# A hybrid S5 / sparse-attention trunk: the adaLN blocks get other places in a hand-written filling plan

## Chip, core and metric

One NeuronCore of a Trainium2 chip runs the whole program. The metric is the device time of one execution in microseconds (us). The kernel before takes 1371.88 us (median of 3 runs, 1369.35 to 1375.03).

## What is computed

Two layers over a residual stream x of 256 positions and 2048 channels. Layer 0 is an S5 state-space mixer, layer 1 a native-sparse-attention mixer (NSA). Every sub-layer is preceded by an RMSNorm whose output is modulated by a conditioning vector c (adaLN). Cut to what matters:

```
c_act = silu(c)
shift, scale, gate = split(c_act @ mod_w[layer] + mod_b[layer], 3)     # layers 0 and 1
h = rmsnorm(x) * (1 + scale) + shift
# layer 0
u, z = split(h @ w_in, 2)
y = gelu(scan(u) + d_skip * u)            # diagonal complex state space, 128 groups
x = x + gate * ((y * sigmoid(y @ w_glu + b_glu) * silu(z)) @ w_out)
# seam: shared keys and values
kv_shift, kv_scale = split(c_act @ kv_mod_w + kv_mod_b, 2)
kv = (rmsnorm(x) * (1 + kv_scale) + kv_shift) @ w_kv        # then compressed blocks
# layer 1
q, gates, z = split(h1 @ w_qg); o = sum(gates * silu(z) * attention branches)
x = x + gate1 * (o @ w_o);  result = rmsnorm(x)
```

The adaLN products are matrix times vector: every 128 outputs need a 2048 x 128 block of weights, 1 MB, used once.

## The kernel before, in words

**Layout.** x is held transposed, 128 channels by 256 positions in each of 16 tiles. A projection (project, L235) makes 128 outputs from 16 tiles: its weights come in two halves of 512 KB on SP's queue (load_w, L187), each half is split into a high and a low part, 4 tiles at a time (split_w, L195: ACT writes hi at L203, DVE writes lo at L204), and TensorE does three matmuls per tile (L231 to L233): 48 matmuls of 128x256 for one block.

**The ring.** All weights, those of the projections and those of adaLN, go through one pool of 8 buffers of 512 KB (raw_tile, L95; bufs=8 at L77). A transfer is issued when a buffer is free. The hi and lo tiles have 4 buffers each (L78).

**adaLN blocks have two forms.** Columns of c_act @ mod_w needed by the first projection (32 blocks) are made in the prologue. The other 96 blocks are spread over the rest of the kernel:

- dve_mod (L138), letter "d": one block on VectorE. Two transfers of 512 KB on SP's queue, and for each a scalar_tensor_tensor in place over 128x1024 with an accumulated sum (L145). It takes two ring buffers until DVE has used them. It needs cact, the broadcast silu(c), which is loaded and made at L546 and L547, inside the S5 stage.

```
            for e in range(2):
                r = raw_tile()
                nc.sync.dma_start(r, mt[i][:, 8 * e:8 * e + 8, :])
                rf = r.rearrange("p a b -> p (a b)")
                nc.vector.scalar_tensor_tensor(out=rf, in0=rf, scalar=1.0, in1=cact[:, 1024 * e:1024 * e + 1024],
                                               op0=OP.mult, op1=OP.mult,
                                               accum_out=modw[:, col - 32:col - 31] if e else modv[:, col:col + 1])
```

- pe_mod (L169), letter "m": a pair of blocks on TensorE (pe_mod_pair, L150). Four transfers of 512 KB, 32 matmuls of 128x128 (L158; fp32, so the trace counts 64), a copy by ACT (L161), two small matmuls (L163), two bias additions by ACT (L166). There is one PSUM tile for it, so one pair follows the other.

The constants NA and NB (L40) say how many of the 32 blocks for the keys and values, and of the 32 for layer 1's shift and scale, are made in pairs; PE_MODS and DVE_MODS are the orders in which they are made. In all there are 8 pairs and 80 "d".

**Stages.** Prologue with the first 8 blocks of u (to about 157 us in the trace). S5 stage: the u blocks that are left (letter "u", one half of a projection), a turn of u into the scan's layout by 32 KB transfers that ACT and POOL issue (u_turn, L555 to L561), scan_in (L601, TensorE), scan_run (L630, a chain on DVE), scan_local, a second turn and the same for the second half (f=1), scan_out (L677), y_turn (L698), y_split; meanwhile the z blocks ("z", one half each). Then a loop over the z blocks that are left (L738), GLU (16 projections, L746), output (16 projections, L762), the norm between the layers (the seam, L778 to L783), 24 key/value projections (L917) with 8 pieces of compression ("c") and 16 rows of the first q blocks ("q", L886), 12 q projections (L977), 16 heads (L986), and the last projection.

**The plan.** fill() (L596) is called at 119 places; each call takes the next string of PLAN (L59) and issues its letters there:

```
    def fill():
        for c in PLAN[slot[0]]:
            {"u": u_half, "z": z_half, "m": pe_mod, "d": dve_mod, "c": lambda: cmp_next(), "q": lambda: q_rows()}[c]()
        slot[0] += 1
```

The string behind the second turn and that of the z loop are two of them; the loop spreads its "m" and "d" over its blocks (L736). Deadlines are caught up in code: 16 "d" before the output stage (L757), all blocks for keys and values before the seam (L771 to L774), and in q_rows the blocks that its row needs (L894 to L898):

```
        while npe[0] < NA + min(NB, 2 * k + 2):
            pe_mod()
        if 2 * k >= NB:
            while ndve[0] < 48 - NA + 2 * k + 2 - NB:
                dve_mod()
```

The text's order is a priority: the framework that builds the program puts an instruction ahead of an earlier one on the same engine where it expects the earlier one to wait. On the chip each engine then runs its instructions in the order so fixed.

Of the kernel before, what the change touches and what calls it, by code (L numbers as in the profile page):

```python
# [36 lines left out]

NA, NB = 12, 4  # L40
L1 = [t for k in range(16) for t in (48 + k, 64 + k)]
PE_MODS = list(range(96, 96 + NA)) + L1[:NB]
DVE_MODS = list(range(32, 48)) + list(range(96 + NA, 128)) + L1[NB:] + list(range(80, 96))
# [3 lines left out]
def spread(n, slots, a=0):  # L47
# [9 lines left out]


PLAN = [  # L59
# [1106 lines left out]
```

## Time and profile before

| what | value |
|---|---|
| median of 3 runs | 1371.88 us (1369.35 to 1375.03) |
| profiled execution, device time | 1371.4 us |
| its span, first to last instruction | 1369.4 us |
| busy PE / DVE / ACT | 1262.9 / 1060.8 / 675.8 us |
| read from HBM | 324.79 MB |
| mean granted TensorE clock | 0.962 of full speed |

The profiled execution lies 0.5 us under the median; 2.0 us of it are outside the span. Busy time of PE is that of pipelined matmuls whose ends are modelled, so what PE can do is better read from the spacing of its starts.

### The profile page before, as it was taken

To read this page: it belongs to the slowest core of one execution; us is meant where nothing else is said; L and a number is where in the kernel's file an instruction comes from. 1 tells how busy PE (TensorE), PEld (TensorE's weight loads), DVE (VectorE), ACT (ScalarE), POOL (GpSimd) and SP (SyncE) were. 2 spreads that over 40 slices of the span, in tenths; PEclk is the share of its full clock that TensorE was granted. 3 is DMA by queue.
4 is the path that set the end of the run, shared out by engine and by line. 5 is a ranking of instruction groups with operands and counts; after the bars stand their busy time and mean duration, and the time that the engine had idled before them with its cause. 6 is when DMAs were issued, how large, how long until landed. Compare 5 with 4: busy or idle time off the path is not lost.

```text
span 1369.4 us, 31323 instructions
## 1 busy us (share of the span) xinstructions
PE 1262.9 (92%) x12266; PEld 1211.3 (88%) x12266; DVE 1060.8 (77%) x2303; ACT 675.8 (49%) x1446; POOL 66.7 (5%) x139
## 2 busy tenths in 40 slices
PE   2799989799989999988998899999999999999994
PEld 1687889798889999988998899999999999999994
DVE  5999558889867887879876789877888777776664
ACT  3255554336454555444444455555555556565652
POOL 2000224120010000000000000000000000000001
PEclk9899989899999999998889999999999999999997
DMA  9799864447888999988886789876565444444541
GB/s 341 253 378 316 317 213 149 123 161 249 306 281 285 344 367 368 367 332 297 274 264 219 237 287 369 314 270 227 176 200 195 145 155 151 144 153 155 185 139 62
DMA packets 97347, 334.43 MB, mean 244 GB/s; under 512 B 14560, under 2 KB 15488, under 8 KB 96176
## 3 DMA queue, kind: packets, MB, share of 16 engines
q1 hardware_dynamic: 91792, 321.45, 66.9%
q0 software_dynamic: 4384, 9.94, 2.2%
q8 instruction: 96, 1.57, 0.5%
q10 hardware_dynamic: 1024, 1.05, 0.3%
q14 instruction: 51, 0.42, 0.1%
HBM read 324.79 MB, written 4.19 MB: 240 GB/s over the span
## 4 chain that ended last, share of the span: by engine, by line
PE 75%; DMA 10%; DVE 9%; issue 3%; ACT 2%; ACTq 1%; SPq 0%; DVEq 0%
PE acc L233 20%; PE acc L231 20%; PE acc L232 19%; DMA raw<-in_mt_dram 5%; DVE lo L204 2%; PE macc L158 2%; DMA mraw<-in_m0n_dram 2%; DVE raw L145 2%; PE s L1000 1%; PE tp L670 1%; PE vp L612 1%; PE op L1051 1%; DMA U<-x 1%; PE uacc L302 1%; ACTq L561 1%
## 5 line engine op out<-in xcount | busy, mean ns | idle before, releaser
L203 ACT ACTIVATE hi<-raw 128x512 fp32r<-128x512 f32 x640 | 398.7, 630 | 464.0 <-PE acc L232 395.4
L204 DVE TENSOR_TENSOR lo<-raw,hi 128x512 fp32r<-128x512 f32 x640 | 431.8, 687 | 144.6 <-ACT hi L203 139.3
L232 PE MATMUL acc<-hq,hi 128*128 128x256 f32 x960 | 274.2, 286 | 0.0
L231 PE MATMUL acc<-hq,hi 128*128 128x256 f32 x960 | 273.1, 285 | 0.0
L233 PE MATMUL acc<-hq,lo 128*128 128x256 f32 x960 | 270.4, 283 | 0.0
L145 DVE SCALAR_TENSOR_TENSOR raw<-raw,ey 128x1024 f32<-128x1024 f32 x160 | 194.6, 1220 | 54.5 <-DMA raw<-in_mt_dram 51.9
L232 PEld LDWEIGHTS acc<-hq,hi 128*128 128x128 f32 x960 | 181.0, 188 | 3.6 <-issue 3.3
L231 PEld LDWEIGHTS acc<-hq,hi 128*128 128x128 f32 x960 | 181.0, 189 | 1.0 <-issue 1.0
L233 PEld LDWEIGHTS acc<-hq,lo 128*128 128x128 f32 x960 | 180.3, 189 | 0.7 <-issue 0.7
L233 PE MATMUL acc<-hkv,lo 128*128 128x256 f32 x384 | 116.9, 305 | 11.0 <-DVE lo L204 10.9
L232 PE MATMUL acc<-hkv,hi 128*128 128x256 f32 x384 | 114.8, 300 | 4.9 <-DVE hkv L266 4.7
L231 PE MATMUL acc<-hkv,hi 128*128 128x256 f32 x384 | 115.2, 301 | 3.6 <-ACT hi L203 3.3
L233 PE MATMUL acc<-h,lo 128*128 128x256 f32 x384 | 112.6, 294 | 4.0 <-DVE lo L204 4.0
L231 PE MATMUL acc<-h,hi 128*128 128x256 f32 x384 | 114.2, 298 | 0.0
L232 PE MATMUL acc<-h,hi 128*128 128x256 f32 x384 | 111.3, 290 | 0.0
L233 PEld LDWEIGHTS acc<-hkv,lo 128*128 128x128 f32 x384 | 79.7, 208 | 14.2 <-DVE lo L204 13.8
L232 PEld LDWEIGHTS acc<-hkv,hi 128*128 128x128 f32 x384 | 79.4, 207 | 6.3 <-DVE hkv L266 6.3
L231 PEld LDWEIGHTS acc<-hkv,hi 128*128 128x128 f32 x384 | 79.4, 207 | 4.9 <-ACT hi L203 4.9
L233 PEld LDWEIGHTS acc<-h,lo 128*128 128x128 f32 x384 | 75.4, 197 | 6.4 <-DVE lo L204 5.0
L158 PE MATMUL macc<-mraw,cz 128*32 128x128 f32 x1536 | 57.2, 300 | 24.0 <-DMA mraw<-in_m0n_dram 20.0
L231 PEld LDWEIGHTS acc<-h,hi 128*128 128x128 f32 x384 | 75.8, 197 | 2.5 <-issue 1.0
L232 PEld LDWEIGHTS acc<-h,hi 128*128 128x128 f32 x384 | 75.9, 198 | 0.2 <-issue 0.2
(332 smaller groups left out, 2827.0 us busy)
## 6 DMA issues: line engine op xcount, KB each, us to landing
raw<-in_mt_dram SPq DMA_DIRECT2D x160, 512.0 KB, 6.0
raw<-in_w_z_dram SPq DMA_DIRECT2D x96, 512.0 KB, 3.8
mraw<-in_m0n_dram SPq DMA_DIRECT2D x64, 512.0 KB, 8.0
raw<-in_w_in_dram SPq DMA_DIRECT2D x48, 512.0 KB, 4.4
raw<-in_w_kv_dram SPq DMA_DIRECT2D x48, 512.0 KB, 5.0
mraw<-in_mn_dram SPq DMA_DIRECT2D x32, 512.0 KB, 6.0
raw<-in_w_glu_dram SPq DMA_DIRECT2D x32, 512.0 KB, 5.8
raw<-in_w_out_dram SPq DMA_DIRECT2D x32, 512.0 KB, 7.5
```

The source lines that it names most:

```text
L145: nc.vector.scalar_tensor_tensor(out=rf, in0=rf, scalar=1.0, in1=cact[:, 1024 * e:1024 * e + 1024], op0=OP.mult, op1=OP.mult, accum_out=mo ...
L158: nc.tensor.matmul(acc[32 * j:32 * j + 32, 128 * e:128 * e + 128], cz[:, q, :], r[:, q % 8, :], start=(e == 0 and q < 4), stop=(q >= 12), ...
L203: nc.scalar.activation(hi[:, 0:c, :], rr, AF.Copy)
L204: nc.vector.tensor_sub(lo[:, 0:c, :], rr, hi[:, 0:c, :].bitcast(F32))
L231: nc.tensor.matmul(acc, hi[:, kk, :], act(0, k), start=(k == 0), stop=False)
L232: nc.tensor.matmul(acc, hi[:, kk, :], act(1, k), start=False, stop=False)
L233: nc.tensor.matmul(acc, lo[:, kk, :], act(0, k), start=False, stop=(k == KT - 1))
L302: nc.tensor.matmul(acc, hi[:, i % 4, :], h0(0, k), start=(k == 0 and i % 2 == 0), stop=False, skip_group_check=True)
L561: (nc.gpsimd if e else nc.scalar).dma_start(U[o:o + 16, f, g], ucm[f][32 * g + 16 * e:32 * g + 16 * e + 16, j])
L612: nc.tensor.matmul(p[e][64 * g2:64 * g2 + 64, hl, r, :], VH[pr, r, h].rearrange("p b m -> p (b m)")[:, 64 * g2:64 * g2 + 64], U[pr, f, 2 * ...
L670: nc.tensor.matmul(p[pr, m, :], tz[pr, hl].rearrange("p d n m -> p (d n) m")[:, :, m], U[pr, f, 2 * g2 + hl, m, :], start=(m == 0), stop=T ...
L1000: nc.tensor.matmul(sp, qo(a, h)[:, qs], kk[:, kv, b, o:o + w], start=(i == 0), stop=(i == 2))
```

## The change

Two constants and the first half of the plan change; no function does. NA goes from 12 to 8 and NB from 4 to 8: of the 16 blocks that are made in pairs, 4 move from the keys and values to layer 1, and as many the other way among the "d". The number of pairs (8) and of "d" (80) stays.

```diff
-NA, NB = 12, 4
+NA, NB = 8, 8
 PLAN = [
-    "uduudu", "u", "u", "u", "u", "uuuu", "uu", "uu", "zzzz", "z", "z", "z", "z", "z", "z", "zzzz", "zz",
-    "z", "z", "z", "z", "zz", "d", "d", "d", "", "d", "", "d", "zzzzddddm",
-    "d", "d", "d", "d", "m", "d", "d", "d", "d", "d", "m", "d", "d", "d", "d", "m",
-    "d", "d", "d", "d", "m", "d", "d", "d", "d", "m", "d", "d", "d", "", "d", "",
-    "mm",
+    "ududuududu", "ud", "u", "ud", "u", "uudu", "uu", "ud", "zzdzzzzd", "zd", "z", "zd", "z", "zd", "z", "zzdz", "zzd",
+    "z", "zd", "z", "zd", "zz", "d", "d", "d", "", "d", "", "d", "zzzzdddd",
+    "d", "", "d", "", "m", "d", "", "d", "", "d", "m", "d", "", "d", "", "d",
+    "m", "d", "", "d", "d", "", "d", "", "m", "d", "d", "", "d", "", "d", "d",
+    "mmmm",
     "d", "d", "d", "d", "dcd", "dc", "cd", "dcd", "cd", "cd", "cd",
     "cd", "dqq", "dq", "dqq", "dqq", "dq", "dq", "dqq", "dq", "dq", "qq", "q", "q",
```

Counting the letters in the order of the calls, with the catching up of q_rows:

| stage | "d" before | "d" after | pairs before | pairs after |
|---|---|---|---|---|
| S5, to the last y_split | 7 | 22 | 0 | 0 |
| z loop | 4 | 4 | 1 | 0 |
| GLU | 13 | 8 | 3 | 2 |
| output | 12 | 9 | 2 | 2 |
| seam | 0 | 0 | 2 | 4 |
| keys, values, q rows | 28 | 23 | 0 | 0 |
| q projections | 10 | 10 | 0 | 0 |
| heads | 6 | 4 | 0 | 0 |

The 5 "d" fewer in the key/value stage are those that q_rows caught up before, 3 at its block 21 and 2 at block 22. Behind the first turn 6 halves of u stand instead of 4, behind the second 6 halves of z instead of 4; from there on one or two halves more have been issued at each place until the z loop.

## Rows read from the trace of the kernel before

**Rows 1.** Windows: us; PE, PEld, DVE, ACT, POOL busy (count), PEclk, DMA share, GB/s.

```profile
157.00:188.00 31.00, 25.71 (x285) 24.18 (x284) 15.29 (x61) 14.43 (x28) 17.07 (x35) 0.83 0.57 183
188.00:398.00 210.00, 194.43 (x2559) 184.37 (x2559) 177.55 (x321) 96.97 (x187) 36.66 (x79) 0.95 0.63 212
300.00:336.00 36.00, 36.00 (x412) 33.40 (x411) 34.96 (x75) 22.55 (x40) 4.32 (x9) 1.00 0.69 229
336.00:398.00 62.00, 54.05 (x737) 50.73 (x736) 51.65 (x96) 28.95 (x50) 4.92 (x13) 0.94 0.85 300
398.00:440.00 42.00, 39.26 (x369) 38.30 (x368) 29.88 (x56) 21.45 (x40) 0.00 (x0) 1.00 0.77 259
440.00:603.00 163.00, 162.62 (x1586) 159.70 (x1584) 128.81 (x237) 80.24 (x153) 0.00 (x0) 1.00 0.94 357
603.00:660.00 57.00, 46.45 (x360) 42.92 (x357) 54.12 (x111) 28.24 (x57) 0.00 (x0) 0.86 0.87 310
...
790.00:850.00 60.00, 57.44 (x466) 55.80 (x467) 52.92 (x113) 28.81 (x61) 0.00 (x0) 1.00 0.93 322
850.00:1353.00 503.00, 501.51 (x4093) 491.44 (x4091) 372.46 (x945) 281.43 (x656) 0.00 (x0) 1.00 0.54 182
```

**Rows 2.** Waits of DVE, 188 to 398 us: in total, times, longest.

```profile
DVE lo L204 <- ACT hi L203: 18.5, 17, 2.8
DVE raw L145 <- DMA raw<-in_mt_dram: 8.5, 5, 3.2
```

**Rows 3.** Timeline of DVE: first and last of scan_run's 16 correction steps.

```profile
312.67 1.08 DVE L658 TENSOR_TENSOR scr<-scr,stab 128x896 f32<-128x896 f32 x1
...
377.88 1.08 DVE L659 TENSOR_TENSOR Vvb<-Vvb,scr 128x896 f32<-128x896 f32 x1
```

**Rows 4.** Timeline of DVE: first "d"; start, us, what [idle before].

```profile
188.52 1.22 DVE L145 SCALAR_TENSOR_TENSOR raw<-raw,ey 128x1024 f32<-128x1024 f32 x1 [2.53 <-ACT ey L547]
...
189.67 1.22 DVE L145 SCALAR_TENSOR_TENSOR raw<-raw,ey 128x1024 f32<-128x1024 f32 x1
```

**Rows 5.** L145 between 188 and 398 us, all instances.

```profile
L145 DVE SCALAR_TENSOR_TENSOR raw<-raw,ey x26: 1206/1218/1362, 188.5 to 393.1; 128x1024 f32<-128x1024 f32 x26
```

**Rows 6.** Waits of PE, 150 to 410 us.

```profile
PE vp L612 <- DMA U<-x: 12.4, 5, 3.9
...
PE macc L158 <- DMA mraw<-in_mn_dram: 2.4, 1, 2.4
```

**Rows 7.** Timeline of ACT in the same stretch.

```profile
161.17 4.31 ACTq L561 DMA_DIRECT2D U<-x  x5
...
171.57 2.17 ACT L203 ACTIVATE hi<-raw 128x512 fp32r<-128x512 f32 x4
```

**Rows 8.** Timeline of PE behind the first turn of u.

```profile
175.24 1.72 PE L612 MATMUL vp<-U,Vva 64*64 64x64 f32 x26 [3.91 <-DMA U<-x]
176.90 0.58 PE L231 MATMUL acc<-h,hi 128*128 128x256 f32 x1
```

**Rows 9.** Timeline of PE: end of the output stage and seam.

```profile
600.81 0.28 PE L232 MATMUL acc<-ghl,hi 128*128 128x256 f32 x1
600.93 0.28 PE L233 MATMUL acc<-ghl,lo 128*128 128x256 f32 x1
601.14 1.95 PE L158 MATMUL macc<-mraw,cz 128*32 128x128 f32 x64
...
603.60 0.61 PE L163 MATMUL macc<-ones,msum 128*128 128x1 f32 x4
...
607.66 0.38 PE L231 MATMUL acc<-hkv,hi 128*128 128x256 f32 x1 [1.00 <-ACT hi L203]
```

**Rows 10.** Timeline of SP's queue at the seam: issues.

```profile
585.28 12.11 SPq L156 DMA_DIRECT2D mraw<-in_mn_dram  x8
601.85 1.75 SPq L191 DMA_DIRECT2D raw<-in_w_kv_dram  x2
```

**Rows 11.** The page: GB/s in 40 slices of the span.

```profile
GB/s 341 253 378 316 317 213 149 123 161 249 306 281 285 344 367 368 367 332 297 274 264 219 237 287 369 314 270 227 176 200 195 145 155 151 144 153 155 185 139 62
```

## Prediction

> **What bounds the kernel now.** I read the windows by stage first, to see which engine is full where [rows 1]. In GLU and output (398 to 603 us) TensorE is: 39.26 of 42 us and 162.62 of 163 us are busy, while DVE has 12.1 and 34.2 us to spare. From 850 us on it is full too, 501.51 of 503 us. In the S5 stage (188 to 398 us) no engine is full: PE 194.43, DVE 177.55 of 210 us. At the end of the key/value stage (790 to 850 us) both nearly are: PE 57.44, DVE 52.92 of 60 us. So a "d" block, which is DVE work, is free in GLU and output, and the question is what it costs in S5.
>
> Next the waits of DVE in S5 [rows 2] and one chain of its timeline. Its idle time there is not a free hole: 18.5 us of it are the lo parts waiting for ACT, in 17 pieces, 8.5 us "d" blocks waiting for their data. The 16 correction steps that end scan_run of the second half are 1.08 us each, 17.3 us in all, but run from 312.67 to 378.96 us [rows 3]; "d" blocks, lo parts and y splits stand between them. Behind them come scan_out, y_turn and y_split of that half, and GLU needs all 16 y tiles before it can finish one block. So what DVE has in its queue ahead of the last correction step delays the end of the stage. DVE sets it, with PE close behind.
>
> **Part by part. "d" blocks in S5.** The two instructions of a block start 1.15 us apart [rows 4], so one block is 2.30 us of DVE. By 398 us 26 had run, 13 blocks [rows 5], though the plan has 11 up to the end of the z loop: the order on DVE runs two blocks ahead of the text. After the change the plan has 22 up to the last y_split and 26 with the loop. If the loop's four slip into GLU, 9 blocks are added before 398 us, 20.7 us; if the lead of two stays, 15 blocks, 34.5 us. I take 12, 27.6 us. With the 177.55 us there now that is 205.2 us of work. How full can DVE get? From 300 to 336 us it is 34.96/36, 97%, from 300 to 398 us 86.61/98, 88%, both with "d" blocks at hand to fill it [rows 1]. I take the middle, 0.927: 221.3 us, that is +11.3 us. The ends: 198.25/0.97 gives -5.6, 212.05/0.884 gives +29.9 us. With the cover gone every further block costs 2.30/0.927, 2.5 us.
>
> **More u and z at the turns.** PE waits 12.4 us in all for the transfers of the two turns [rows 6]; that is the most that more u and z could win. I count nothing. The new halves need their hi part from ACT, and ACT's queue is issuing the turn's transfers: five of them take from 161.17 to 165.48, the last hi work before is over, and the next four hi parts start at 171.57 [rows 7]. PE's order has the scan's matmuls first, at 175.24 after 3.91 us of waiting, and u behind them at 176.90 [rows 8]: u that was already in the plan did not fill this wait. There is a bound on the other side. The first slot now has four "d" blocks, which take all 8 ring buffers until cact is there; the first L145 waits for it until 188.52 [rows 4]. Halves of u behind them can't be loaded meanwhile. PE could lose 188.52 - 176.90, 11.6 us. Ends: -12.4 and +11.6, taken 0, as the row of u at 176.90 is nearest to what the plan asks for.
>
> **The pair out of the z loop.** A pair is 1.95 us of L158 and 0.61 us of L163 on PE [rows 9], 2.56 us, and this one made PE wait 2.4 us for its data [rows 6]. PE does not set the end of this stage alone: between 0 and -5.0, taken -2.
>
> **GLU and output.** One pair less, -2.56 us; PE's idle time there is 42 - 39.26 + 163 - 162.62, 3.1 us [rows 1], of which fewer transfers may give back half: -4 in all. The 8 "d" blocks that leave give nothing themselves, since PE covers them.
>
> **Seam.** Two more pairs are 5.1 us of PE. They issue 8 more transfers on SP's queue; before, 8 for two pairs fill the ring from 585.28 on, and the first key/value weights are issued at 601.85, when the first pair frees buffers [rows 10]. Now pairs three and four come there first, 4.2 MB, at 357 GB/s [rows 1] 11.7 us, and behind them wait the key/value weights and the first "d" blocks. PE is idle for 57 - 46.45, 10.6 us from 603 to 660 us, and DVE is full there, 54.12 of 57, with the norm, whose work can go on while the weights are late. So 0 if DVE bounds this stretch, +11.7 if the weights do; taken +5, the matmuls alone, since PE's idle time and the late weights pull in opposite ways.
>
> **Key/value end.** Five "d" blocks fewer at blocks 21 and 22, 11.5 us of DVE, but PE has only 2.6 us of idle time to win there [rows 1]: between 0 and -5, taken -2. The q_rows additions that go with NB (two blocks' worth of small adds) are inside that. **Heads:** two blocks fewer under a full PE, 0.
>
> **Sum:** 11.3 + 0 - 2 - 4 + 5 - 2 = +8.3 us. Against the profiled execution's 1371.4 us that is 1379.7; it lies 0.5 under the median of 1371.88, so 1380 as a median, 0.6% slower. A measurement of this kernel tells 0.5%, 6.9 us, from no change.
>
> **Rivals.** *No change, 1373.* The loop's four blocks slip into GLU and the lead of two is lost, so that only 9 blocks are added: 198.25/0.927 is 213.9, +3.9 us, and the sum +0.9. For it: the order on the engines is not the text's, and DVE in GLU has room. Against: the lead of two seen now.
>
> *Faster, 1358.* The transfers, not PE, hold GLU and output, and the turns are half filled. From 440 to 603 us 357 GB/s are moved, DMA share 0.94 [rows 1]. PE's own need there is 32 blocks of 48 matmuls at 0.12 us apart [rows 9], 184.3 us, and four pairs, 10.2: 194.5 of now 205 us. If fewer transfers let it reach that, -10.5; the turns give -6; with DVE 97% full S5 costs 205.2/0.97, +1.5; the rest as above, -2 + 5 - 2: -14. It decides if S5 grows by less than 4 us. Against it: slices of the same span move 367 to 378 GB/s [rows 11], more than 357, so the transfers have some room left, and PE shows only 3.1 us of idle time there.
> The Trainium skill states in "DMA: Bandwidth & Descriptors", Specifications, a limit of about 358 GB/s of HBM per core; by it this stage would stand at its limit, and the 10.5 MB taken out of it would be worth, as an estimate, 29 us, cut to the 10.5 that PE allows. The slices of 367 to 378 GB/s lie above that figure. The skill's "Perfetto Trace Analysis", Optimization Strategy, also advises to interleave stretches that lean on different engines; by that rule this rival is right, as S5 moves 212 GB/s only. The row of DVE in S5 speaks against it: the engine that "d" needs besides the transfers is 85% busy there.
>
> *Slower still, 1392.* The ring is held by the four early "d" blocks, u comes late, the second turn with it: +11.6 on top of the forecast. For it: 8 buffers, and cact at 188.52. Against: ACT may make cact earlier if its order changes, and DVE has 15.7 us idle from 157 to 188 us [rows 1].
>
> **Chances.** Forecast 0.33, no change 0.28, faster 0.27, slower still 0.12. Slower by over 0.5%: 0.28 of the forecast's, all of the last and 0.02 of the second, 0.42. Faster: 0.22 of the third and 0.04 of the second, 0.26. Within: the remaining 0.32. The range goes from 1357, just under the faster case, to 1398: the forecast with two thirds of the further 18.6 us that S5's upper end allows, 1392 included. The forecast's own range is 1374 to 1392.
>
> **What would show it.** S5: the first GLU matmul, now near 398 us, comes near 409; DVE over 92% busy from 188 us to there, with some 50 L145 before it. Turns: PE still waits about 12 us for U. GLU and output: about 201 us instead of 205. Seam: from the last matmul of the output to the first on hkv 13 us or more instead of 6.7 [rows 9]. Key/value end: PE idle under 2 us. I'm wrong if S5 ends before 402 us, if PE's waits for U fall under 6 us, or if GLU and output take 195 us.

## Result and profile after

The changed kernel takes 1387.3 us (median of 4 runs, 1382.08 to 1387.65), the kernel before, timed beside it on the same chip, 1370.74 (1369.35 to 1375.03): 1.0107 times as long, 95% interval 1.0073 to 1.014. It is slower by more than a measurement can miss. Ratios and intervals, here and below, are those on record for the repeated runs; they differ a little from the quotient of two medians. The profiled execution took 1387.09 us, its span is 1385.2.

The 15.8 us between the two spans are the sum of larger terms of both signs. The table takes them from the trace, by the starts of matmuls: the prologue ends with the last one on uacc, S5 and GLU with the last one that reads yhl, the output with the last one on ghl, the seam with the first one on hkv, the key/value stage with the last one on hkv. What is left behind the last matmul on hkv is the rest. The experiments below have their rows in the same table, under the labels of their recorded expectations.

| kernel | prologue | S5 and GLU | output | seam | key/value | rest | span |
|---|---|---|---|---|---|---|---|
| before | 157.6 | 342.6 | 100.7 | 6.7 | 237.5 | 524.3 | 1369.4 |
| changed | 160.7 | 370.9 | 100.2 | 17.5 | 207.1 | 528.8 | 1385.2 |
| e1_s5_strings | 157.8 | 368.1 | 101.2 | 6.7 | 225.4 | 525.6 | 1384.8 |
| e2_seam_pairs | 158.3 | 340.9 | 97.4 | 25.0 | 206.3 | 527.4 | 1355.3 |
| e3_uz_moves | 156.6 | 340.4 | 100.7 | 6.7 | 237.9 | 524.3 | 1366.8 |
| e4_short_sums | 158.3 | 353.3 | 99.9 | 17.2 | 205.3 | 527.6 | 1361.7 |
| e5_no_loads | 158.4 | 354.3 | 101.2 | 17.9 | 202.2 | 529.0 | 1363.0 |
| e6_late_d | 156.1 | 375.2 | 100.5 | 19.1 | 198.5 | 527.8 | 1377.2 |
| e7_no_late_d | 159.4 | 348.0 | 102.4 | 22.5 | 202.9 | 527.6 | 1362.8 |
| e8_load_ahead | 159.5 | 366.8 | 100.9 | 17.7 | 203.7 | 529.0 | 1377.6 |
| e9_two_in_seam | 155.9 | 369.7 | 100.1 | 10.9 | 226.4 | 527.7 | 1390.7 |
| e10_early_40 | 157.7 | 336.5 | 103.0 | 18.7 | 208.3 | 528.1 | 1352.2 |
| e11_after_ring7 | 164.3 | 369.3 | 103.6 | 18.5 | 212.0 | 527.8 | 1395.4 |
| e12_before_ring7 | 162.5 | 335.7 | 101.9 | 8.5 | 241.8 | 526.9 | 1377.2 |

Each row is one execution. Kernels with the S5 plan of before differ in S5 and GLU by some 6 us either way (335.7 to 348.0), so only more than that is read from the table; the whole times come from the repeated runs.

S5 and GLU lose 28 us, the seam 11, the rest 4.5, the prologue 3 (it varies by more from trace to trace); the key/value stage wins 30; the output stage is unchanged. The windows of the changed kernel, as in [rows 1] (us; PE, PEld, DVE, ACT, POOL busy and instructions; PE's clock, DMA share, GB/s):

```profile
188.00:424.00 236.00, 205.03 (x2380) 194.07 (x2379) 209.19 (x369) 94.17 (x178) 31.70 (x66) 0.91 0.75 252
401.00:436.00 35.00, 29.23 (x470) 26.83 (x469) 27.46 (x39) 8.11 (x15) 0.00 (x0) 0.66 0.60 205
436.00:532.00 96.00, 93.66 (x827) 90.79 (x826) 66.08 (x129) 51.55 (x102) 4.21 (x13) 1.00 0.74 255
532.00:632.00 100.00, 98.38 (x918) 96.10 (x916) 72.50 (x134) 46.82 (x86) 0.00 (x0) 1.00 0.87 304
632.00:650.00 18.00, 12.21 (x263) 9.02 (x262) 14.71 (x36) 10.51 (x27) 0.00 (x0) 0.88 0.91 332
```

GLU and output are as full on PE as before, at 255 and 304 GB/s instead of 324 (398 to 500 us) and 357: fewer transfers there gave nothing. The loss is between 401 and 436 us. The timeline of PE (start, us, what [idle before]):

```profile
410.72 0.28 PE L233 MATMUL acc<-yhl,lo 128*128 128x256 f32 x1
414.26 1.08 PE L158 MATMUL macc<-mraw,cz 128*32 128x128 f32 x16 [3.26 <-DMA mraw<-in_mn_dram]
415.27 6.52 PE L688 MATMUL yp<-Vvb,ct 64*64 64x64 f32 x128
...
423.94 6.31 PE L688 MATMUL yp<-Vvb,ct 64*64 64x64 f32 x120 [0.73 <-DVE Vvb L659]
430.18 5.52 PE L704 MATMUL yt<-U,stab 128*32 128x128 f32 x124
435.63 0.39 PE L231 MATMUL acc<-yhl,hi 128*128 128x256 f32 x1
```

GLU's first 48 matmuls read the first eight y tiles only and run from 401 to 411 us. Then no GLU matmul starts for 24.9 us: y of the second half is not there. It waits for the last correction step of scan_run; timeline of DVE:

```profile
422.79 1.09 DVE L659 TENSOR_TENSOR Vvb<-Vvb,scr 128x896 f32<-128x896 f32 x1
```

Before, it started at 377.88 us [rows 3]. That is 45 us. Before, GLU began 20.3 us behind the step, as PE still had z to do; now it goes on 12.8 us behind it, with 48 matmuls (5.7 us) done: 45 - 7.5 - 5.7 = 32 us arrive. What DVE does up to the end of that step is the key to this case. The groups of DVE lines, before (188 to 379 us) and then after (188 to 424), busy time, mean ns | idle before them:

```profile
L204 DVE TENSOR_TENSOR lo<-raw,hi 128x512 fp32r<-128x512 f32 x79 | 53.3, 685 | 17.1 <-ACT hi L203 16.7
L145 DVE SCALAR_TENSOR_TENSOR raw<-raw,ey 128x1024 f32<-128x1024 f32 x23 | 27.7, 1216 | 6.8 <-DMA raw<-in_mt_dram 4.2 <-ACT ey L547 2.5
```

```profile
L145 DVE SCALAR_TENSOR_TENSOR raw<-raw,ey 128x1024 f32<-128x1024 f32 x56 | 67.8, 1221 | 22.9 <-DMA raw<-in_mt_dram 20.3 <-ACT ey L547 2.5
L204 DVE TENSOR_TENSOR lo<-raw,hi 128x512 fp32r<-128x512 f32 x94 | 62.9, 686 | 3.7 <-ACT hi L203 2.8 <-DMA raw<-in_mt_dram 0.7
```

33 more L145, 40.1 us, and 15 more lo parts, 9.6 us, stand ahead of the last step. The busy time of the window grows by less than their sum, 44.7 us: the list counts each instruction in full, and successive ones overlap (the two L145 of a block start 1.15 us apart and take 1.22). The window of before that belongs to it, DVE being the third busy time:

```profile
188.00:379.00 191.00, 177.83 (x2304) 168.85 (x2303) 164.54 (x290) 86.79 (x169) 31.74 (x66) 0.96 0.60 202
```

Before, 191 - 164.54 = 26.5 us idle; after (first row of the windows above), 236 - 209.19 = 26.8. The whole of the added work lengthened the stretch up to the last step, and none of the idle time took it up. That time changed its cause instead: before, DVE waits for ACT's hi parts, after, for the data of "d" itself.

### The profile page after: what moved, and what is told of

It reads as the page before. It is cut to its first block, busy times and chain, and to the rows that moved or that the text cites. A ratio compares the mean times of both kernels' runs of the same rounds, so it can differ in the third digit from the quotient of the medians.

```text
span 1385.2 us, 31312 instructions
## 1 busy us (share of the span) xinstructions
PE 1266.0 (91%) x12266; PEld 1213.8 (88%) x12266; DVE 1061.9 (77%) x2299; ACT 674.9 (49%) x1445; POOL 65.9 (5%) x139
## 4 chain that ended last, share of the span: by engine, by line
PE 69%; DMA 13%; DVE 12%; issue 3%; ACT 2%; SPq 0%; ACTq 0%; DVEq 0%; POOL 0%
PE acc L233 19%; PE acc L231 18%; PE acc L232 18%; DMA raw<-in_mt_dram 8%; DVE lo L204 3%; DVE raw L145 2%; DMA mraw<-in_m0n_dram 2%; PE macc L158 1%; PE s L1000 1%; PE op L1051 1%; PE yp L688 1%; PE tp L670 1%; PE op L1048 1%; PE vp L612 1%; PE yt L704 1%
## 5 line engine op out<-in xcount | busy, mean ns | idle before, releaser
L145 DVE SCALAR_TENSOR_TENSOR raw<-raw,ey 128x1024 f32<-128x1024 f32 x160 | 194.8, 1221 | 73.1 <-DMA raw<-in_mt_dram 70.1
L233 PE MATMUL acc<-hkv,lo 128*128 128x256 f32 x384 | 112.7, 294 | 1.4 <-DVE lo L204 1.2
L231 PE MATMUL acc<-hkv,hi 128*128 128x256 f32 x384 | 112.5, 293 | 0.9 <-ACT hi L203 0.9
L232 PE MATMUL acc<-hkv,hi 128*128 128x256 f32 x384 | 111.5, 291 | 0.0
L231 PEld LDWEIGHTS acc<-h,hi 128*128 128x128 f32 x384 | 75.3, 196 | 6.7 <-ACT hi L203 5.1
L233 PEld LDWEIGHTS acc<-hkv,lo 128*128 128x128 f32 x384 | 76.4, 199 | 2.8 <-DVE lo L204 2.6
L231 PEld LDWEIGHTS acc<-hkv,hi 128*128 128x128 f32 x384 | 76.8, 200 | 1.3 <-ACT hi L203 1.3
L233 PE MATMUL acc<-yhl,lo 128*128 128x256 f32 x256 | 74.1, 291 | 4.1 <-DVE lo L204 4.0
L232 PEld LDWEIGHTS acc<-hkv,hi 128*128 128x128 f32 x384 | 76.8, 200 | 0.0
```

Source lines behind the costliest of these rows:

```text
L231: nc.tensor.matmul(acc, hi[:, kk, :], act(0, k), start=(k == 0), stop=False)
L232: nc.tensor.matmul(acc, hi[:, kk, :], act(1, k), start=False, stop=False)
L233: nc.tensor.matmul(acc, lo[:, kk, :], act(0, k), start=False, stop=(k == KT - 1))
```

## Experiments

**The S5 strings alone.**

```diff
-    "uduudu", "u", "u", "u", "u", "uuuu", "uu", "uu", "zzzz", "z", "z", "z", "z", "z", "z", "zzzz", "zz",
-    "z", "z", "z", "z", "zz", "d", "d", "d", "", "d", "", "d", "zzzzddddm",
+    "ududuududu", "ud", "u", "ud", "u", "uudu", "uu", "ud", "zzdzzzzd", "zd", "z", "zd", "z", "zd", "z", "zzdz", "zzd",
+    "z", "zd", "z", "zd", "zz", "d", "d", "d", "", "d", "", "d", "zzzzddddm",
```

> The kernel before with the S5 strings of the changed kernel alone (22 "d" and its u and z moves); z loop, GLU, output and a seam of two pairs as before. The 80 "d" are used up earlier, so the five that were caught up at the end of the key/value stage and some of the heads' fall away. Theory ("d" in S5 is work in DVE's chain): the last GLU matmul comes some 31 us later than before (500 to about 531 us), as in the changed kernel, though GLU has all its 13 "d" again. The key/value stage tells two rivals apart: if it was shortened by the five "d" that are no longer caught up there, it takes about 210 us instead of 237, and the whole 1375 to 1380; if it was shortened by the four pairs in the seam, it stays at 237, and the whole is about 1400.

1385.34 us against 1370.79, ratio 1.0086 (1.0059 to 1.0114). S5 and GLU take 368.1 us, 25.5 more than before, with all of GLU's "d" back in place; GLU ends 25.6 us later than before, where 31 were expected. So the S5 strings carry the loss. The key/value stage came out between the two expectations, 225.4 us: the "d" that are no longer caught up there explain 12 of the 30.

**The seam alone.** The S5 strings stay as before. NA, NB and the four pairs of the seam are those of the changed kernel; the pair of the z loop and one of GLU go, three "d" more stand in GLU and output, and output's two pairs come earlier.

```diff
-NA, NB = 12, 4
+NA, NB = 8, 8
-    "z", "z", "z", "z", "zz", "d", "d", "d", "", "d", "", "d", "zzzzddddm",
-    "d", "d", "d", "d", "m", "d", "d", "d", "d", "d", "m", "d", "d", "d", "d", "m",
-    "d", "d", "d", "d", "m", "d", "d", "d", "d", "m", "d", "d", "d", "", "d", "",
-    "mm",
+    "z", "z", "z", "z", "zz", "d", "d", "d", "", "d", "", "d", "zzzzdddd",
+    "d", "d", "d", "d", "m", "d", "d", "d", "d", "d", "m", "d", "d", "d", "d", "d",
+    "m", "d", "d", "d", "d", "d", "d", "d", "m", "d", "d", "d", "d", "d", "d", "d",
+    "mmmm",
```

> The kernel before with NA = NB = 8 and four pairs in the seam; S5 strings as before, the pair of the z loop and one of GLU taken out, "d" in the freed and two empty places so that 39 are made by the seam. One "d" is still caught up at the key/value end, not five. If the pairs in the seam shorten the key/value stage, seam and key/value stage together take 20 us less, as in the changed kernel, and without the S5 cost the whole is about 1350. If they only lengthen the seam, it is 1371 + 11 less what four fewer caught-up "d" give (9 us at most), 1373 to 1382.

1356.82 us, ratio 0.9877 (0.9849 to 0.9905): faster than both kernels. Seam and key/value stage take 231.3 us instead of 244.2, 13 less where 20 were expected, and output 97.4 with more "d" than before, at 365 GB/s and a DMA share of 0.97 (440 to 600 us, PE 157.99 of 160 us busy). The seam itself is 25 us, longer than in the changed kernel. A block that is caught up stands ahead of the norm there; timeline of DVE:

```profile
597.65 1.21 DVE L145 SCALAR_TENSOR_TENSOR raw<-raw,ey 128x1024 f32<-128x1024 f32 x1
...
598.79 0.42 DVE L248 TENSOR_TENSOR tot<-tot,sq 128x256 f32<-128x256 f32 x1
...
600.50 1.75 DVE L256 RECIPROCAL rstd<-rstd 128x256 f32<-128x256 f32 x1 [0.78 <-ACT rstd L255]
```

**The u and z moves alone.**

```diff
-    "uduudu", "u", "u", "u", "u", "uuuu", "uu", "uu", "zzzz", "z", "z", "z", "z", "z", "z", "zzzz", "zz",
+    "uduuduuu", "u", "u", "u", "u", "uuu", "uu", "u", "zzzzzz", "z", "z", "z", "z", "z", "z", "zzz", "zz",
```

> The kernel before with only the u and z halves moved as in the changed kernel, the 7 "d" of S5 where they were. Theory: the moves cost and bring little, 1371 +- 4, and the first GLU matmul and the last one stay within 4 us of before (398 and 500 us). Rival (the moved halves are what makes S5 long): GLU ends 10 us later or more, the whole 1381 or more. A second rival (they fill the turns): PE's wait for U falls under 6 us from 12.4, the whole 1365 or less.

1370.9 against 1370.79, ratio 0.999 (0.9963 to 1.0016): nothing. PE's wait for U is 7.8 instead of 12.4 us in this trace, but no stage is shorter for it. By themselves the moves are out as a cause of the loss.

**No "d" ahead of the second turn.** In the changed kernel the eight "d" of the first eight strings go behind the turn.

```diff
-    "ududuududu", "ud", "u", "ud", "u", "uudu", "uu", "ud", "zzdzzzzd", "zd", "z", "zd", "z", "zd", "z", "zzdz", "zzd",
-    "z", "zd", "z", "zd", "zz", "d", "d", "d", "", "d", "", "d", "zzzzdddd",
+    "uuuuuu", "u", "u", "u", "u", "uuu", "uu", "u", "zzddzzdzzd", "zd", "zd", "zd", "zd", "zd", "zd", "zzdz", "zzd",
+    "zd", "zd", "zd", "zd", "zz", "d", "d", "d", "d", "d", "", "d", "zzzzdddd",
```

> The changed kernel with the eight "d" that stand ahead of the second turn moved behind it (still 22 in S5, none of them holds ring buffers before cact is made). Rival (the early "d" hold the ring until cact is there, and u and the second turn come late): GLU ends 10 us earlier or more, and the whole is about 1375. Theory (each "d" costs its DVE work wherever in S5 it stands): GLU ends within 5 us of the changed kernel's 532, the whole 1383 to 1391.

1383.1 us, ratio 1.0081 (1.0053 to 1.0109). The second turn comes back to its old time (first matmul on the second half's U at 241.9 us, 254.0 in the changed kernel, 243.6 before), and still GLU ends at 531.3, as in the changed kernel (531.6). Early blocks do delay the turn, but that doesn't set the end. As many "d" lie ahead of the last correction step, 56 L145 here too, and that step starts at 423.9 us.

**DVE's work or the transfers?** Two counterparts, one with the transfers and hardly any work, one with the work and no transfers, for 15 of the 22 blocks. The first leaves most of 15 products out of the output, the second all of them.

```diff
-                rf = r.rearrange("p a b -> p (a b)")
+                n = 64 if 2 <= i < 17 else 1024
+                rf = r.rearrange("p a b -> p (a b)")[:, 0:n]
...
-in1=cact[:, 1024 * e:1024 * e + 1024],
+in1=cact[:, 1024 * e:1024 * e + n],
```

> The changed kernel in which 15 of the "d" blocks of S5 (the third to the seventeenth) multiply and sum only 64 of 1024 columns of each half: all transfers and ring buffers stay, nearly all DVE work of these blocks goes (the output leaves out most of 15 adaLN products). Theory (DVE work in the chain): GLU ends near where it does in the kernel before, 500 to 508 us instead of 532. Rival (ring and transfers, or the wait for their data in DVE's queue): GLU still ends at 520 or later.

```diff
-                nc.sync.dma_start(r, mt[i][:, 8 * e:8 * e + 8, :])
+                if not 2 <= i < 17:
+                    nc.sync.dma_start(r, mt[i][:, 8 * e:8 * e + 8, :])
...
-in0=rf,
+in0=cact[:, 0:1024] if 2 <= i < 17 else rf,
```

> The counterpart: the changed kernel in which the same 15 blocks keep their DVE work and their ring buffers but load nothing (DVE multiplies a constant tile; the output leaves out 15 adaLN products). Theory (DVE work): GLU ends within 6 us of the changed kernel's 532, at most the 37 us that "d" waited for data fall and turn into other idle time. Rival (waits for data): GLU ends at 510 or earlier. In either case the 15.7 MB not loaded leave S5's transfers well under its limit.

One run each, 1363.6 us with the short sums and 1364.93 without the loads. GLU ends at 511.6 and 512.7 us, between 500.2 before and 531.6 in the changed kernel: both expectations fell in both. The windows up to the last correction step, first of the one, then of the other (DVE is the third busy time):

```profile
188.00:397.00 209.00, 185.19 (x2302) 173.96 (x2302) 173.19 (x359) 87.96 (x170) 31.68 (x66) 0.96 0.78 260
```

```profile
188.00:408.00 220.00, 203.81 (x2388) 193.11 (x2382) 200.64 (x356) 95.41 (x180) 31.64 (x66) 0.91 0.59 195
```

Work plus idle time makes the stretch in each: 173.2 + 35.8, 200.6 + 19.4, and in the changed kernel 209.2 + 26.8. With the data in place, DVE takes 36 us more work than before with 7 us less idle time, and is 91% full. With the loads and hardly any work it idles 9 us more than before. The last correction step starts at 395.9 us with the short sums and at 406.8 without the loads: 18 us later than before by the loads alone, 29 by the work alone, 45 by both. In DVE's chain the two add up, within the 5 us by which this step varies among traces of one S5 plan (373.7 to 382.9 us with that of before).

GLU's end shows less of each, 11 and 12 of 31 us. Before, PE had z to do until 20.3 us behind the step; GLU runs without a break from 404.9 us with the short sums, from 416.8 without the loads and from 435.6 in the changed kernel, 9.0, 10.0 and 12.8 us behind it. So 8 to 11 us of a delay are covered by work that PE has anyway, and in each kernel they are covered once; without the loads and in the changed kernel GLU's first 50 and 48 matmuls, done early, cover 6 us more. With the short sums 7 us are left of the 18, and GLU itself takes some 5 us longer. How much of the loads' 18 us is late data, and how much the buffers and the queue that they take from u and z, was not tried apart.

**Can the data come earlier?** First by asking one block ahead in S5 (until the z loop; load_mod issues the two transfers of a block), then by the ring.

```diff
+    def load_mod(i):
...
+            while len(loaded) < 1 + ahead[0] and i + len(loaded) < len(DVE_MODS):
+                loaded.append(load_mod(i + len(loaded)))
-            for e in range(2):
-                r = raw_tile()
-                nc.sync.dma_start(r, mt[i][:, 8 * e:8 * e + 8, :])
+            for e, r in enumerate(loaded.pop(0)):
```

> The changed kernel, but in S5 each "d" first issues the two transfers of the next "d", so that a block's data is asked for one "d" ahead of its DVE work. The fourth and fifth experiments put 11 to 12 us each on the late data and on the DVE work of the added blocks. Theory (late data: DVE, in its fixed order, waits for a block's transfer with the scan's steps behind it): DVE's waits for the data of "d" up to 532 us fall from 35.6 to under 18 us, GLU ends at 515 to 526 instead of 532, the whole 1372 to 1382. Rival (the ring: two more of its 8 buffers are held, so the u and z halves come later): GLU ends at 532 or later, the whole 1387 or more.

1386.67 us, ratio 1.0118 (1.0086 to 1.0151), the same as the changed kernel. DVE's waits for "d" up to 532 us are 33.7 us (35.6 in the changed kernel): 2 us went where 18 were expected to. GLU ends at 526.3 us in its trace, that of the fastest of its four executions (1379.6 us); the median shows no gain. Asking earlier in the text did not bring the data earlier.

```diff
-    ring = ctx.enter_context(tc.tile_pool(name="ring", bufs=8))
+    ring = ctx.enter_context(tc.tile_pool(name="ring", bufs=7))
```

> The changed kernel with 7 buffers in the ring instead of 8. Theory (in S5 the data of "d" is late because SP can't issue before DVE gives a buffer back, and DVE waits for the data that SP has not issued): with one buffer less this loop is slower; DVE's waits for the data of "d" up to 532 us rise from 35.6 to 45 us or more, and the last correction step of the second half comes 5 to 15 us later than the changed kernel's 423. Rival (8 buffers are enough, the data is late because the transfers themselves are slow): the last correction step comes within 3 us of 423, the waits stay at 32 to 39.

> The control: the kernel before with 7 buffers. Theory (only with many "d" in S5 does the ring decide there): the last correction step of the second half comes within 3 us of 378, and what the time grows by comes from GLU and output, where the weights need 340 GB/s or more. Rival (the ring holds S5 in any case): the last correction step comes 5 us later or more here too.

Waits of DVE with 7 buffers in the changed kernel, 160 to 532 us:

```profile
DVE raw L145 <- DMA raw<-in_mt_dram: 32.3, 18, 6.4
```

The last correction step starts at 424.8 us, against 422.8 with 8 buffers, and at 379.8 against 377.9 in the kernel before. So the theory of a loop through the ring fell; one buffer less moves that step by no more than its spread. The two single runs took 1397.38 and 1379.17 us. What they lose in their traces lies in the prologue (3.6 and 4.9 us) and the key/value stage (4.9 and 4.3), with the changed kernel's output 3.4 longer too; that the loss of the kernel before would come from GLU and output did not hold. More buffers were not tried. Why the data of "d" is late stays open.

**Four pairs or two in the seam.** The changed kernel with

```diff
-    "mmmm",
+    "mm",
```

> The changed kernel with two pairs in the seam instead of four; the other two are then made where q rows 2 and 3 ask for them, inside the key/value stage. The number of "d" in each stage stays. Theory (the pairs in the seam run while DVE makes the norm, and that is a part of the key/value stage's gain): the seam takes about 7 us instead of 17.5, the key/value stage 230 or more instead of 207, both together some 8 us more than the changed kernel's 225; the whole 1392 to 1398. Rival (only the five "d" that are no longer caught up shorten the stage): seam and stage together stay at 225 or fall, the whole 1380 to 1388.

1393.49 us, ratio to before 1.0176 (1.0144 to 1.0208); the changed kernel had 1.0107. Seam and key/value stage take 237.3 us instead of 224.6. The groups of L145 in that stretch, before (601 to 846 us), changed (632 to 857), with two pairs in the seam (626 to 863), and in the first experiment (627 to 860):

```profile
L145 DVE SCALAR_TENSOR_TENSOR raw<-raw,ey 128x1024 f32<-128x1024 f32 x60 | 73.2, 1220 | 29.6 <-DMA raw<-in_mt_dram 29.6
```

```profile
L145 DVE SCALAR_TENSOR_TENSOR raw<-raw,ey 128x1024 f32<-128x1024 f32 x52 | 63.4, 1219 | 15.3 <-DMA raw<-in_mt_dram 15.2
```

```profile
L145 DVE SCALAR_TENSOR_TENSOR raw<-raw,ey 128x1024 f32<-128x1024 f32 x52 | 63.5, 1221 | 33.9 <-DMA raw<-in_mt_dram 33.7
```

```profile
L145 DVE SCALAR_TENSOR_TENSOR raw<-raw,ey 128x1024 f32<-128x1024 f32 x52 | 63.5, 1221 | 29.5 <-DMA raw<-in_mt_dram 29.2
```

Two causes come apart. Four blocks fewer (the plan said five) are 9.8 us of DVE work. The other is the wait for the data of "d", 15.2 us with four pairs in the seam, 33.7 with two. The first experiment, with two pairs and 52 L145, has 29.2. So the two further pairs cost 6.6 us in the seam (17.5 against 10.9) and give 19.3 back behind it (207.1 against 226.4), of which 5.1 are the time that they themselves take on PE. Why "d" waits less behind them was not tried.

**A better version.** Two further plans on the second experiment: four more "d" in GLU and output, beside the letters that stand there; and one more in GLU, with the two at the end of the output moved beside its pairs.

```diff
-    "d", "d", "d", "d", "m", "d", "d", "d", "d", "d", "m", "d", "d", "d", "d", "d",
-    "m", "d", "d", "d", "d", "d", "d", "d", "m", "d", "d", "d", "d", "d", "d", "d",
+    "d", "d", "d", "d", "md", "d", "d", "d", "d", "d", "md", "d", "d", "d", "d", "d",
+    "md", "d", "d", "d", "d", "d", "d", "d", "md", "d", "d", "d", "d", "d", "d", "d",
```

> The second experiment (four pairs in the seam, S5 as before) with four more "d" in GLU and output, so that none is caught up ahead of the seam or at the key/value end: 43 by the seam. If the "d" caught up ahead of the norm delays the seam (first matmul on hkv 25 us after the output's last one, instead of 17.5 in the changed kernel), the seam falls by 4 to 7 us and the key/value stage by 2 to 3, and GLU and output grow by the 4 MB of transfers, 0 to 11 us at the 365 GB/s they move there: 1350 to 1360, against about 1357.

```diff
-    "d", "d", "d", "d", "m", "d", "d", "d", "d", "d", "m", "d", "d", "d", "d", "d",
-    "m", "d", "d", "d", "d", "d", "d", "d", "m", "d", "d", "d", "d", "d", "d", "d",
+    "d", "d", "d", "d", "m", "d", "d", "d", "d", "d", "m", "d", "d", "d", "d", "dd",
+    "md", "d", "d", "d", "d", "d", "d", "d", "md", "d", "d", "d", "d", "d", "", "",
```

> The second experiment with its 40th "d" in GLU instead of being caught up right ahead of the norm, and no "d" in the last two output places; the same number of blocks in every other stage. If a "d" between the last output block and the norm holds the seam, seam and key/value stage fall by 2 to 5 us from 231 and the whole is 1351 to 1355. If the transfers of GLU (365 GB/s) take it back, 1355 to 1360.

The first takes 1359.58 us, ratio 0.9923 (0.9901 to 0.9945); its trace is that of the slowest of its six executions (1364.82 us). Seam and key/value stage fall by 5.9 us, but S5, GLU and output grow by 12. The seam itself falls by 2.6 us only, where 4 to 7 were expected: the block caught up ahead of the norm is not all that makes it long. From 440 to 600 us the second experiment, and then this one:

```profile
440.00:600.00 160.00, 157.99 (x1466) 155.30 (x1469) 137.35 (x253) 78.55 (x149) 0.00 (x0) 1.00 0.97 365
```

```profile
440.00:600.00 160.00, 152.79 (x1386) 149.65 (x1385) 135.85 (x247) 77.05 (x151) 0.00 (x0) 0.99 0.97 371
```

At 371 GB/s PE has 7.2 us of idle time in the same 160 us, at 365 GB/s it has 2.0. ACT's hi parts wait 26.4 us for weights in this stretch, against 9.4 in the second experiment. So the room for "d" in GLU and output ends near here; that the transfers alone set the pace is not shown, as from 520 to 560 us PE is 39.91 of 40 us busy at 384 GB/s. The other version takes 1355.46 us, ratio 0.9909 (0.9881 to 0.9937), with a seam of 18.7 us instead of 25, and seam and key/value stage 4.3 us shorter, as expected; the whole can't be told from the second experiment (1356.82). Both are faster than before, and 1355.46 is 2.3% under the changed kernel's 1387.3.

## Why the prediction was right, and where not

The forecast was slower, 1380 us within 1357 to 1398; 1387.3 came. The mechanism of S5 was right. Four terms and a mark were not, and that their sum came within 8 us of the measured time is luck: S5 and GLU, the seam and the rest came out longer than forecast, the key/value stage 28 us shorter.

**"d" in S5, +11.3, mis-sized.** Measured, S5 and GLU together take 28.3 us longer, which stands against +11.3, the -2 of the pair out of the z loop and the -2.56 of GLU's pair. Two choices were wrong in the same direction. Twelve further blocks were taken; by the last correction step there were 33 more L145, 16.5 blocks, so DVE's lead on the text stayed. And DVE was taken to fill to 92.7%, a middle that leaned on the 97% between 300 and 336 us [rows 1]; it reached 88.6%, 209.19 of 236 us. Between 300 and 336 us "d" waited for its data once, 0.7 us; in the changed kernel it waited 20.3 us up to the last step. The upper end, 15 blocks at 88.4% and +29.9, is close to what happened. That DVE would be "over 92% busy" was wrong for this reason.

**The mark for the end of S5.** GLU's first matmul was to come near 409 us, and under 402 the forecast was to be wrong. It came at 401.2, and yet S5 was 31 us late: that matmul needs the first half of y alone. The mark is where GLU runs without a break, 435.6 us. The count was right (54 L145 up to 401 us, some 50 expected).

**Turns, 0.** Right: PE waits 13.5 us for U (before 12.4 [rows 6]), and the moves alone change nothing. The "slower still" rival named a true effect, the second turn 10.4 us late behind the early blocks, and priced it wrongly: without it (e6_late_d) the end is the same.

**GLU and output, -4.** The output stage is 100.2 instead of 100.7 us: nothing. The faster rival fell with it. At the 357 GB/s of before the transfers did not hold these stages. At about 370, in the last experiments, PE begins to wait, so the idea has its place at a higher load. The Trainium skill ("DMA: Bandwidth & Descriptors", Specifications) puts the limit at about 358 GB/s for a core; the measured 365 GB/s over 160 us, with PE 157.99 us busy, lie above it. The Trainium skill's advice to interleave stretches that lean on different engines ("Perfetto Trace Analysis", Optimization Strategy) speaks for moving "d" from GLU to S5, and the trace decides against it here: it cost 28 us and freed none.

**Seam, +5, mis-sized.** It grew by 10.8 us, near the upper bound of 11.7. The two added pairs were priced at their matmuls, 2.56 us each. But there is one PSUM tile, and the next pair starts only after ACT has read it twice; timeline of PE:

```profile
634.20 0.61 PE L163 MATMUL macc<-ones,msum 128*128 128x1 f32 x4
635.31 1.95 PE L158 MATMUL macc<-mraw,cz 128*32 128x128 f32 x64 [0.50 <-ACT modv L166]
638.41 0.61 PE L163 MATMUL macc<-ones,msum 128*128 128x1 f32 x4 [1.15 <-ACT msum L161]
```

From one L163 to the next it is 4.2 us, 8.4 for two pairs. 1.7 us more are waits for the data of the third and fourth pair, the trouble with the queue that the upper bound stood for.

**Key/value end, -2, the term that failed most.** The stage fell by 30.4 us. The prediction looked at the last 60 us, found 2.6 us of idle PE [rows 1] and called that all there was to win (there PE is idle 1.1 us now, as said). But the blocks that go were spread over the stage (60 L145 before, 52 after), and in the stretch of the L145 groups above PE was idle 25.5 of 245 us, and is idle 14.6 of 225 now; before and changed:

```profile
601.00:846.00 245.00, 219.51 (x1715) 210.02 (x1715) 198.35 (x402) 112.88 (x226) 0.00 (x0) 0.90 0.81 275
```

```profile
632.00:857.00 225.00, 210.36 (x1829) 203.09 (x1829) 188.30 (x376) 113.60 (x228) 0.00 (x0) 0.95 0.86 300
```

The same lines show a part that nobody had counted: PE's busy time falls by 9.1 us too, though two more pairs ran in the stretch. The granted clock is 0.95 there instead of 0.90. It is 0.90 to 0.92 in the three traces with the plan of before for this stage; why it rises was not tried. And the pairs in the seam gave back more than their own time, which was not considered at all. The stage's gain hid two thirds of what the others lost, so the total stayed near the forecast.

**Heads, 0.** The rest is 4.5 us longer. It goes with the constants, 524.3 to 526.9 us in the four traces with NA = 12 and 527.4 to 529.0 in all with NA = 8; 1.2 us of it are some 10 matmuls of the last q row, which run behind the last one on hkv now; the cause of the other part was not tried and stays open.

## What to carry to other kernels

When work is added to an engine that runs in a fixed order, count all of it up to the last step that others wait for, and keep that engine's idle time as it is unless the new work's data is known to lie ready: idle time waits for something, and new work that itself waits does not fill it. A part of a delay can hide behind what the next engine still has to do, so half of a change can look cheaper than it is. Take as the end of a stage the point from which the next runs without a break, and price a removed block over the whole stretch in which it can stand, not at the last place of the plan. Move such work by the room that each stage has left in its own limit (here: GLU and output, with PE still full at 365 GB/s), and keep it out of the stage whose chain runs on the same engine.

## What was not expected of the hardware

The pause in GLU costs more than its length. PE has no work from 411 to 414 us, and from 414 to 434 the granted clock is 0.50, the lower level of 1.2 GHz, while steps of the chain run; window of the changed kernel:

```profile
414.00:434.00 20.00, 19.01 (x356) 17.56 (x360) 12.85 (x17) 2.75 (x5) 0.00 (x0) 0.50 0.50 181
```

128 yp matmuls take 6.52 us there, and the 120 behind the last correction step, on the way to GLU, 6.31. In the kernel before, these 120 start within 3.3 us (line L688: durations, first and last start):

```profile
L688 PE MATMUL yp<-Vvb,ct x120: 218/218/267, 379.2 to 382.5; 64*64 64x64 f32 x120
```

The same holds in the seam: the 64 matmuls of a pair take 1.95 us in the changed kernel, where the clock is 1.00 from 632 to 645 us, and 3.64 in the second experiment, where PE had waited 1.76 and 3.03 us ahead of them and the clock is 0.50. In the last version a pair takes 1.95 us again, and the small matmuls L163 0.61 us instead of 1.01. For three pairs that is 6.3 us, about what its seam is shorter, 18.7 instead of 25 us. The second experiment's window and its PE line:

```profile
605.00:620.00 15.00, 11.58 (x175) 9.78 (x178) 10.73 (x30) 8.68 (x22) 0.00 (x0) 0.50 0.95 336
```

```profile
605.95 3.64 PE L158 MATMUL macc<-mraw,cz 128*32 128x128 f32 x64 [0.50 <-ACT modv L166]
```
